# Hybrid decoder layer on one core: transposes of both heads in one row, next scores directly behind, filling steps regrouped

## Chip, core and metric

The kernel runs on one core of one Trainium2 chip. Its time is the device time of one execution in microseconds; several executions are taken and their median is compared. The profile is one execution recorded by the hardware profiler. TensorE is called PE in its rows, its weight loads PEld, VectorE DVE, ScalarE ACT, GpSimd POOL and SyncE, which issues the DMAs, SP.

## The reference

One decoder layer on x of 512 tokens by 1024 channels. The part that matters here is the stick-breaking attention with 8 heads of 64 channels, computed for blocks of 128 queries:

```
for blk in range(S // SB_BLOCK):
    z = jnp.einsum('bthd,bshd->bhts', qb, kb).astype(jnp.float32) * scale
    log_not = jnp.where(strict, jax.nn.log_sigmoid(-z), 0.0)
    suffix = lax.cumsum(log_not, axis=3, reverse=True) - log_not
    a = jnp.where(strict, jnp.exp(jax.nn.log_sigmoid(z) + suffix), 0.0)
    outs.append(jnp.einsum('bhts,bshd->bthd', a, vb))
...
merged = gates0 * (o_sb @ w_br_sb) + gates1 * (o_pool @ w_br_pool) + gates2 * (o_gm @ w_br_gm)
x = x + rms_norm(merged @ w_out, g_mix_post)
x = x + rms_norm(square(relu(rms_norm(x, g_ff_pre) @ w_ff_in)) @ w_ff_out, g_ff_post)
```

Two more mixers (pooling over trailing windows, gMLP gating), three sigmoid gates and a squared-ReLU MLP stand beside it.

## The kernel before, in words

Every float32 operand of a matrix product is cut into a high part (a cast on ACT, names such as whi, hT0, a) and a low part (a subtraction on DVE, wlo, hT1), and each product is three matmuls. One step of the generator `work` is such a product: three matmuls with 512 columns for most of it. `work` chains the projections of the other mixers (gating, pooling), the q and k projections of later head pairs and the gates. The DVE and ACT work that follows these products (win, pooled, pl, og, sg, kl) is issued when a step has been reached.

`attention` goes through 16 units: unit u is head pair u // 4 and query block i = u % 4, so unit 3 is the last block of head pair 0 and unit 4 the first of head pair 1. A unit passes four stages, for both heads of its pair:

- scores (`stick_scores`): four matmuls into two banks z; then on ACT sigmoids into nb and be, on POOL the causal masks, on DVE a reverse scan of nb and a product into be
- transposes (`stick_transpose`): i + 1 transposes of be by PE for each head into a bank pt; ACT casts pt to the high part of a, DVE subtracts for the low part
- values (`stick_values`): 2(i + 1) matmuls a by v into the bank av, of which there is one buffer
- sum: ACT copies the lower half of av to low, DVE adds it (low), and two DVE additions write the output of; both of these read av, so the next unit's values can't begin before they are done

In a pass of the loop the transposes of unit u - 1, the scores of unit u and the values of unit u - 1 are issued with steps of `work` between them (`fill`), in the numbers of FILLS. PE keeps the order of the program throughout. Ahead of attention, ACT and DVE are set free (`act.on = dve.on = False`): from there the scheduler of the framework puts their instructions in order from its own planning, and on the chip each engine then takes them in that fixed order. So the same edit can move instructions on ACT and DVE that it doesn't name.

The names in the rows are tiles; a helper records every operation, so nearly all rows have line 90.

Of the kernel before, what the change touches and what calls it, by code (L numbers as in the profile page):

```python
# [17 lines left out]
P = 128  # L18
T = 512
D = 1024  # L20
NT = T // P
# [9 lines left out]
AHEAD = 3  # L31
NO_SYNC = mybir.DependencyInfo(mybir.DependencyClass.NoSync, mybir.DependencyReason.DATA)
RAW, HL = 3, 6
FILLS = (2, 1, 3, 5)
LEAD = 36
WARM = 6

# [11 lines left out]
def trunk_layer(ctx: ExitStack, tc: tile.TileContext, x, w_in, w_pool, pool_scale, gm_gain,  # L49
# [27 lines left out]
    def slot(ring, name, dt=F32):  # L77
        return home[0].tile([P, T], dt, name=name, tag=ring, bufs=RINGS[ring])
# [19 lines left out]
    pe, act, dve, sp = (InOrder(e, True) for e in (nc.tensor, nc.scalar, nc.vector, nc.sync))  # L98

    def wide(name, dt=F32R):  # L100
        return sb.tile([P, 2 * T], dt, name=name, tag="wide", bufs=2)
# [153 lines left out]
    def split(src, hi, lo, scale=None):  # L255

        if scale is None:
            act.copy(hi, src)
            dve.tensor_sub(lo, src, hi.bitcast(F32))
        else:  # L260
            act.activation(hi, src, AF.Copy, scale=scale)
            dve.scalar_tensor_tensor(lo, src, scale, hi.bitcast(F32), ALU.mult,
                                           ALU.subtract)
# [68 lines left out]
    def bank(tag, name, dt=F32):  # L332
        return psum.tile([P, T], dt, name=name, tag=tag,
                         bufs={"mm": 3, "z": 2, "tr": 2, "av": 1}[tag])
# [23 lines left out]
    ident = cst.tile([P, P], F32, name="ident")  # L358
# [12 lines left out]
    if True:  # L371
# [31 lines left out]
        two, rs, hns, pts = {}, {}, {}, {}  # L403
        for step in V_ORDER.split():
            what = step.rstrip("0123")
            t, g = ([int(c) for c in step[len(what):]] + [0, 0])[:2]
# [56 lines left out]
        def stick_scores(hp, i):  # L463

            xq, kh, kl = qk[hp]
            n = (i + 1) * P
            tsl = slice(i * P, n)
            zs = [bank("z", "z") for _ in range(2)]
            for j in range(2):
                pe.matmul(zs[j][:, :n], lhsT=xq[j][:, tsl], rhs=kh[j][:, :n], start=True,  # L470
                                 stop=False)
            for j in range(2):
                pe.matmul(zs[j][:, :n], lhsT=xq[j][HALF[j], tsl], rhs=kl[HALF[j], :n],
                                 start=False, stop=True)
            res = []
            for j in range(2):
                nb, be = slot("nb", "nb"), slot("be", "be")
                act.activation(nb[:, :n], zs[j][:, :n], AF.Sigmoid, scale=-0.125)
                act.activation(be[:, :n], zs[j][:, :n], AF.Sigmoid, scale=0.125)

                for tile_, fill in ((nb, 1.0), (be, 0.0)):
                    nc.gpsimd.affine_select(tile_[:, n - P:n], tile_[:, n - P:n], [[-1, P]],  # L482
                                            ALU.is_ge, fill, base=-1, channel_multiplier=1)
                dve.tensor_tensor_scan(nb[:, :n][:, ::-1], nb[:, :n][:, ::-1],
                                             zeros.broadcast_to([P, n]), 1.0, ALU.mult, ALU.add)
                dve.tensor_mul(be[:, :n - 1], be[:, :n - 1], nb[:, 1:n])
                res.append(be)
            return res

        def stick_transpose(i, be):  # L490

            pt = bank("tr", "pt").rearrange("p (s t) -> p s t", s=NT)
            for s in range(i + 1):
                pe.transpose(pt[:, s, :], be[:, s * P:(s + 1) * P], ident)
            a = wide("a").rearrange("p (s a t) -> p s a t", s=NT, a=2)[:, :i + 1]
            split(pt[:, :i + 1, :], a[:, :, 0, :], a[:, :, 1, :])
            return a

        def stick_values(hp, i, parts, of):
            av = bank("av", "av").rearrange("p (j a t) -> p j a t", j=2, a=2)  # L500
            for j in range(2):
                hd = 2 * hp + j
                for s in range(i + 1):
                    vv = vT[s][hd // 4][:, hd % 4, :, :].rearrange("p a d -> p (a d)")
                    pe.matmul(av[:, j, :, :], lhsT=vv, rhs=parts[j][:, s, :, :],
                                     start=s == 0, stop=s == i)
            low = slot("tmp", "low")[:DH, :2 * P].rearrange("p (j t) -> p j t", j=2)
            act.copy(low, av[DH:P, :, 0, :])
            dve.tensor_add(low, av[0:DH, :, 0, :], low)
            for j in range(2):  # L510
                dve.tensor_add(of[HALF[j], i * P:(i + 1) * P], av[0:DH, j, 1, :],
                                     low[:, j, :])

        def attention(fill):

            units = [(hp, i) for hp in range(4) for i in range(NT)]
            be = parts = of = None
            for u in range(len(units) + 1):
                if u:
                    hp0, i0 = units[u - 1]  # L520
                    parts = []
                    for j in range(2):
                        parts.append(stick_transpose(i0, be[j]))
                        fill(FILLS[j])
                if u < len(units):
                    hp, i = units[u]
                    while qk[hp] is None:
                        fill(1)
                    be = stick_scores(hp, i)
                fill(FILLS[2])  # L530
                if u:
                    if i0 == 0:
                        of = slot("tmp", "of")
                    stick_values(hp0, i0, parts, of)
                    if i0 == NT - 1:
                        oT[hp0] = slot("out", "oh", F32R), slot("out", "ol", F32R)
                        split(of, *oT[hp0])
                fill(FILLS[3])


        wsr = slot("tmp", "wsr").rearrange("p (g t) -> p g t", g=4)
# [221 lines left out]
        def fill(n):  # L763
            for _ in range(n):
                next(work, None)
# [4 lines left out]
        pool_constants()  # L770
        fill(LEAD - LEAD // 2)
        attention(fill)
        run(work)
        for dd in range(KD // 2):
# [112 lines left out]
    parts = [None] * (FT // 2)  # L887
# [210 lines left out]
```

## Time and profile before

| | |
|---|---|
| median of 3 runs | 722.36 us (721.77 to 723.73) |
| the profiled execution | 722.87 us |
| its span, first to last instruction | 721.1 us |
| PE busy | 698.6 us, 97% |
| DVE busy | 494.0 us, 68% |
| ACT busy | 353.9 us, 49% |
| attention | from about 72 to 232 us of the span |

Times in rows are us from the start of the span. A timeline row has the start, the time until the end of the row's last instruction, the engine, the operation and its tiles (out<-in), the number of instructions, and in brackets the idle time of the engine before it with what ended it. Ends of matmuls are modelled, so two starts are compared rather than an end and a start.

### The profile page before, as it was taken

Reading aid. Unit: us, or ns where it says so; the run is one execution under the profiler, and the core shown is the slowest. Engines: PE = TensorE matmul, PEld = TensorE weight load, DVE = VectorE, ACT = ScalarE, POOL = GpSimd, SP = SyncE. Lnnn points to the kernel's source line nnn. Section 1 sums busy time; section 2 is a strip of 40 time slices with the busy share of each in tenths; the row PEclk is TensorE's granted clock in tenths of the full one; section 3 lists DMA queues with packets and bytes.
Section 4 is the critical chain, followed back from the end, with each engine's and each line's share of the span. In section 5 each row is a group of like instructions: output and inputs, shape, how many; then the busy total and the mean of one; then the engine's idle time right before and its main releaser. Section 6 shows DMA issues by size and latency. Waiting matters only on the chain.

```text
span 721.1 us, 9135 instructions
## 1 busy us (share of the span) xinstructions
PE 698.6 (97%) x3320; PEld 576.7 (80%) x3320; DVE 494.0 (68%) x771; ACT 353.9 (49%) x593; POOL 54.0 (7%) x106
## 2 busy tenths in 40 slices
PE   7999999999999999999999998999999999999994
PEld 4889887788888888888889777888888888888774
DVE  6745799777777544243576776747885679757897
ACT  6566666655444333321445654555534553445541
POOL 4100222111121000000040000000000000000001
PEclk9999999999999999999999999999999999999998
DMA  8272312322325233262325235633356234643543
GB/s 278 80 207 84 115 60 60 90 68 70 96 59 146 89 90 114 74 220 87 116 89 176 99 106 175 181 113 115 119 165 208 92 117 148 188 133 116 162 160 117
DMA packets 72432, 89.80 MB, mean 125 GB/s; under 512 B 4546, under 2 KB 49730, under 8 KB 72387
## 3 DMA queue, kind: packets, MB, share of 16 engines
q1 hardware_dynamic: 72384, 89.21, 39.5%
q8 instruction: 26, 0.43, 0.2%
q14 instruction: 20, 0.16, 0.1%
q10 hardware_dynamic: 2, 0.00, 0.0%
HBM read 85.01 MB, written 4.19 MB: 124 GB/s over the span
## 4 chain that ended last, share of the span: by engine, by line
PE 80%; DVE 10%; DMA 4%; ACT 3%; issue 2%; POOL 1%; SPq 0%; POOLq 0%; DVEq 0%; ACTq 0%
PE psc L90 25%; PE accf L90 18%; PE accx L90 7%; PE psb L90 6%; PE acc L90 6%; PE accz L90 5%; PE accy L90 4%; PE psv L90 3%; DMA raw<-in_w_ff_out_dram 3%; DVE wlo L90 2%; DVE ys L90 2%; PE psgv L90 2%; PE z L90 1%; PE av L90 1%; PE pt L90 1%
## 5 line engine op out<-in xcount | busy, mean ns | idle before, releaser
L90 DVE TENSOR_TENSOR wlo<-raw,whi 128x1024 fp32r<-128x1024 f32 (+1 forms) x145 | 158.1, 1095 | 109.6 <-ACT whi L90 108.8
L90 ACT CAST whi<-raw 128x1024 fp32r<-128x1024 f32 (+1 forms) x152 | 139.4, 927 | 140.5 <-PE psc L90 31.0
L90 PE MATMUL psc<-hT,whi 128*128 128x512 f32 x576 | 182.2, 398 | 0.0
L90 PE MATMUL accf<-hT,whi 128*128 128x512 f32 x448 | 138.1, 390 | 1.4 <-ACT rl L90 1.4
L90 PEld LDWEIGHTS psc<-hT,whi 128*128 128x128 f32 x576 | 103.9, 188 | 21.0 <-issue 1.5
L90 PE MATMUL psc<-hT,wlo 128*128 128x512 f32 x288 | 112.6, 391 | 0.0
L90 PEld LDWEIGHTS accf<-hT,whi 128*128 128x128 f32 x448 | 84.0, 188 | 19.1 <-ACT rl L90 1.8
L90 PE MATMUL accf<-hT,wlo 128*128 128x512 f32 x224 | 87.2, 389 | 0.0
L90 PEld LDWEIGHTS psc<-hT,wlo 128*128 128x128 f32 x288 | 54.1, 188 | 11.6
L90 PEld LDWEIGHTS accf<-hT,wlo 128*128 128x128 f32 x224 | 42.1, 188 | 8.8
L90 ACT CAST ah<-ec 128x768 fp32r<-128x768 f32 (+1 forms) x32 | 30.2, 944 | 32.6 <-DVE ec L90 32.1
L90 PE MATMUL accx<-whi,ah 128*128 128x512 f32 x96 | 37.9, 394 | 2.9 <-DVE ys L90 2.9
L284 POOL TENSOR_TENSOR pr<-pv,mhalf 128x1 f32<-128x1 f32 x8 | 4.8, 605 | 470.7 <-DVE pv L90 470.7
L90 DVE TENSOR_TENSOR al<-ec,ah 128x768 fp32r<-128x768 f32 (+1 forms) x32 | 34.8, 1087 | 4.7 <-ACT ah L90 4.5
L90 PE MATMUL accx<-wlo,ah 128*128 128x512 f32 x96 | 37.4, 390 | 0.0
L90 PE MATMUL accx<-whi,al 128*128 128x512 f32 x96 | 37.4, 390 | 0.0
L90 DVE TENSOR_TENSOR_SCAN nb<-nb,zeros 128x128 f32<-128x128 f32 (+3 forms) x32 | 27.5, 863 | 7.5 <-POOL nb L482 7.1
L90 DVE TENSOR_TENSOR ec<-ec 128x256 f32<-128x256 f32 x64 | 26.7, 421 | 7.0 <-ACT ec L90 6.7
L90 ACT CAST whi<-t 128x512 fp32r<-128x512 f32 x32 | 19.7, 616 | 14.8 <-DVE t L90 9.2
L90 PE MATMUL accy<-whi,al 128*128 128x512 f32 (+1 forms) x64 | 24.7, 386 | 1.9 <-DVE al L90 1.9
L90 ACT CAST a<-pt 128x128 fp32r<-128x128 f32 (+3 forms) x32 | 13.6, 426 | 25.9 <-PE pt L90 25.8
L90 ACT ACTIVATE sg<-psc 128x512 f32<-128x512 f32 x24 | 14.3, 598 | 22.7 <-PE psc L90 22.7
(197 smaller groups left out, 1236.0 us busy)
## 6 DMA issues: line engine op xcount, KB each, us to landing
raw<-in_w_ff_out_dram SPq DMA_DIRECT2D x96, 256.0 KB, 3.2
raw<-in_w_in_dram SPq DMA_DIRECT2D x42, 512.0 KB, 3.8
raw<-in_w_ff_in_dram SPq DMA_DIRECT2D x32, 512.0 KB, 3.9
xt<-in_x_dram SPq DMA_DIRECT2D x16, 256.0 KB, 6.3
raw<-in_w_out_dram SPq DMA_DIRECT2D x8, 512.0 KB, 3.7
raw<-in_w_ff_out_dram SPq DMA_DIRECT2D x8, 512.0 KB, 3.8
raw<-in_w_br_sb_dram SPq DMA_DIRECT2D x4, 512.0 KB, 3.4
x1d<-xt SPq DMA_DIRECT2D x8, 256.0 KB, 2.7
```

Of the source, the lines that this page charges most:

```text
L90: i = op(*args, **kw).ins
L284: nc.gpsimd.tensor_tensor(r, v, mhalf, ALU.pow)
```

## The change

FILLS has two numbers in place of four. The transposes of both heads are issued in a row, with no steps between them, and the scores of the next unit directly behind. Four steps stand between scores and values, where there were three, and seven behind the values, where there were five; a pass has 11 steps as before. Both banks pt are written before the casts and subtractions are issued. In the first pass, which has no transposes or values, 11 steps stand where there were 8.

```
-FILLS = (2, 1, 3, 5)
+FILLS = (4, 7)
...
-        def stick_transpose(i, be):
-
-            pt = bank("tr", "pt").rearrange("p (s t) -> p s t", s=NT)
-            for s in range(i + 1):
-                pe.transpose(pt[:, s, :], be[:, s * P:(s + 1) * P], ident)
-            a = wide("a").rearrange("p (s a t) -> p s a t", s=NT, a=2)[:, :i + 1]
-            split(pt[:, :i + 1, :], a[:, :, 0, :], a[:, :, 1, :])
-            return a
+        def stick_transposes(i, be):
+
+            pts = [bank("tr", "pt").rearrange("p (s t) -> p s t", s=NT) for _ in range(2)]
+            for j in range(2):
+                for s in range(i + 1):
+                    pe.transpose(pts[j][:, s, :], be[j][:, s * P:(s + 1) * P], ident)
+            res = []
+            for pt in pts:
+                a = wide("a").rearrange("p (s a t) -> p s a t", s=NT, a=2)[:, :i + 1]
+                split(pt[:, :i + 1, :], a[:, :, 0, :], a[:, :, 1, :])
+                res.append(a)
+            return res
...
-                    parts = []
-                    for j in range(2):
-                        parts.append(stick_transpose(i0, be[j]))
-                        fill(FILLS[j])
+                    parts = stick_transposes(i0, be)
...
-                fill(FILLS[2])
+                fill(FILLS[0])
...
-                fill(FILLS[3])
+                fill(FILLS[1])
```

On PE, around the transposes of unit 3 (pt, four per head) and the scores of unit 4 (z), the order before has three matmuls psc, which are one step, on both sides of the second head's transposes:

```order
L90 MATMUL psc<-hT_142,whi 128x512
L90 MATMUL psc<-hT_143,whi 128x512
L90 MATMUL psc<-hT_142,wlo 128x512
L90 MATMUL pt<-ident,be 128x128 x4
L90 MATMUL psc<-hT_142,whi 128x512
L90 MATMUL psc<-hT_143,whi 128x512
L90 MATMUL psc<-hT_142,wlo 128x512
L90 MATMUL z<-kh,xq 128x128 x2
L90 MATMUL z<-kl,xq 128x128 x2
```

The same place in the changed kernel:

```order
L90 MATMUL psc<-hT_142,whi 128x512
L90 MATMUL psc<-hT_143,whi 128x512
L90 MATMUL psc<-hT_142,wlo 128x512
L90 MATMUL pt<-ident,be 128x128 x8
L90 MATMUL z<-kh,xq 128x128 x2
L90 MATMUL z<-kl,xq 128x128 x2
```

The three steps that stood behind the transposes of head 0 now stand ahead of them; the scores keep their place among the steps, and the values of unit 3 come four steps behind them instead of three.

On DVE, before, from the pooling work (pooled) onward: low and of with av_1186 in them are the sum of unit 2; a_1246 and a_1263 are the transposed weights of unit 3; pl, win and wlo belong to the pooling mixer and to the weights:

```order
L90 SCALAR_TENSOR_TENSOR pooled_1216<-win_1176,tok_937 64x512 x2
L90 TENSOR_TENSOR low_1193<-av_1186,low_1193 64x256
L90 TENSOR_TENSOR pooled_1216<-first_1219,tok_937 128x16
L90 TENSOR_TENSOR of_951<-av_1186,low_1193 64x128 x2
L90 TENSOR_TENSOR a_1246<-pt_1241,a_1246 128x4x128
L90 TENSOR_TENSOR pl_1223<-pooled_1216,ph_1222 128x512
L90 TENSOR_TENSOR win_1235<-tok_1008 128x511
L90 COPY win_1235<-tok_1008 128x1
L90 TENSOR_TENSOR a_1263<-pt_1258,a_1263 128x4x128
L90 TENSOR_TENSOR wlo_1452<-raw_1211,whi_1451 128x1024
L90 TENSOR_TENSOR win_1255<-win_1235 128x510
```

In the changed kernel the pair pooled (64x512) is followed by pooled (128x16), pl, win (128x511) and its one-column copy, and then by these rows, where the sum of unit 2 has av_1214 in it, a_1263 and a_1266 are unit 3's, and nb_1275 and nb_1285 are the two scans of unit 4:

```order
L90 TENSOR_TENSOR wlo_1452<-raw_1199,whi_1451 128x1024
L90 TENSOR_TENSOR win_1247<-win_1235 128x510
L90 COPY win_1247<-win_1235 128x2
L90 TENSOR_TENSOR kl_1297<-psc_1194,kh_1295 128x512
L90 TENSOR_TENSOR low_1221<-av_1214,low_1221 64x256
L90 TENSOR_TENSOR a_1263<-pt_1253,a_1263 128x4x128
L90 TENSOR_TENSOR a_1266<-pt_1254,a_1266 128x4x128
L90 SCALAR_TENSOR_TENSOR nb_1275<-nb_1275,zeros_138 128x128
L90 TENSOR_TENSOR win_1317<-win_1247 128x508
L90 COPY win_1317<-win_1247 128x4
L90 SCALAR_TENSOR_TENSOR nb_1285<-nb_1285,zeros_138 128x128
L90 TENSOR_TENSOR of_954<-av_1214,low_1221 64x128 x2
```

The pair of unit 2 that last reads av stood directly behind pooled; it now stands behind pl, wlo, kl, both a of unit 3, the win chain and both scans of unit 4.

On ACT, before, at the same place (xq and kh are casts for the q and k of a later head pair, ph is the high part of pooled):

```order
L90 COPY low_1193<-av_1186 64x256
L90 CAST xq_1199<-psc_1108 64x512
L90 COPY xq_1198<-ql_1200 64x512
L90 COPY xq_1199<-ql_1200 64x512
L90 CAST a_1246<-pt_1241 128x4x128
L90 CAST ph_1222<-pooled_1216 128x512
L90 CAST a_1263<-pt_1258 128x4x128
L90 CAST whi_1451<-raw_1211 128x1024
L90 CAST kh_1295<-psc_1206 128x512
```

and in the changed kernel:

```order
L90 CAST xq_1187<-psc_1108 64x512
L90 COPY xq_1186<-ql_1188 64x512
L90 COPY xq_1187<-ql_1188 64x512
L90 CAST ph_1210<-pooled_1204 128x512
L90 CAST whi_1451<-raw_1199 128x1024
L90 CAST kh_1295<-psc_1194 128x512
L90 COPY low_1221<-av_1214 64x256
L90 CAST a_1263<-pt_1253 128x4x128
L90 CAST a_1266<-pt_1254 128x4x128
```

The copy low of unit 2 moved from ahead of xq to behind kh, and both casts a of unit 3 stand behind it.

## Rows read from the trace of the kernel before

**Rows 1.** The page: span, and busy time by engine.
```profile
span 721.1 us, 9135 instructions
PE 698.6 (97%) x3320; PEld 576.7 (80%) x3320; DVE 494.0 (68%) x771; ACT 353.9 (49%) x593; POOL 54.0 (7%) x106
```

**Rows 2.** What PE waited for in the run: us in total, times, longest.
```profile
PE accx L90 <- DVE ys L90: 2.9, 2, 2.0
...
PE pt L90 <- DVE be L90: 0.4, 1, 0.4
PE av L90 <- DVE a L90: 0.2, 1, 0.2
```

**Rows 3.** Busy time in one stretch: us, PE, PEld, DVE, ACT, POOL, clock, DMA.
```profile
113.43:119.84 6.41, 6.19 (x31) 5.12 (x30) 6.41 (x13) 4.74 (x11) 2.30 (x4) 1.00 0.21 54
```

**Rows 4.** Timeline of PE around unit 3, and the values of unit 15.
```profile
111.41 0.60 PE L90 MATMUL pt<-ident,be 128*128 128x128 f32 x4
...
112.55 0.33 PE L90 MATMUL z<-kh,xq 128*128 128x128 f32 x2
...
115.24 0.63 PE L90 MATMUL av<-a,v 128*128 128x256 f32 x4
...
116.67 0.62 PE L90 MATMUL psc<-hT,whi 128*128 128x512 f32 x2
...
119.84 0.39 PE L90 MATMUL psc<-hT,wlo 128*128 128x512 f32 x1
120.59 0.30 PE L90 MATMUL pt<-ident,be 128*128 128x128 f32 x1 [0.36 <-DVE be L90]
...
230.74 1.12 PE L90 MATMUL av<-a,v 128*128 128x256 f32 x8
231.69 0.40 PE L90 MATMUL psb<-plh,whi 128*128 128x512 f32 x1
```

**Rows 5.** Timeline of DVE around the sum of unit 2.
```profile
110.94 1.38 DVE L90 SCALAR_TENSOR_TENSOR pooled<-win,tok 64x512 f32<-64x512 f32 x2
112.35 0.42 DVE L90 TENSOR_TENSOR low<-av,low 64x256 f32<-64x256 f32 x1
112.69 0.16 DVE L90 TENSOR_TENSOR pooled<-first,tok 128x16 f32<-128x16 f32 x1
112.80 0.58 DVE L90 TENSOR_TENSOR of<-av,low 64x128 f32<-64x128 f32 x2
113.43 0.69 DVE L90 TENSOR_TENSOR a<-pt,a 128x512 fp32r<-128x512 f32 x1
...
119.84 0.41 DVE L90 TENSOR_TENSOR low<-av,low 64x256 f32<-64x256 f32 x1
```

**Rows 6.** Timeline of ACT in the same stretch.
```profile
111.54 1.25 ACT L90 CAST xq<-ql 64x512 fp32r<-64x512 f32 x2
...
113.42 0.62 ACT L90 CAST ph<-pooled 128x512 fp32r<-128x512 f32 x1
...
114.43 1.05 ACT L90 CAST whi<-raw 128x1024 fp32r<-128x1024 f32 x1
```

**Rows 7.** Timeline of POOL: the mask of unit 4's second nb.
```profile
117.97 0.29 POOL L482 TENSOR_SCALAR_AFFINE_SELECT nb<-nb 128x128 f32<-128x128 f32 x1
```

**Rows 8.** Timeline of PE at the start of the run.
```profile
1.79 2.74 PE L90 MATMUL warm<-warm 128*128 128x512 bf16 x6 [1.79 <-DVE warm L90]
...
6.90 0.65 PE L90 MATMUL trx<-ident,hn 128*128 128x128 f32 x4 [0.27 <-DVE hn L90]
10.35 0.74 PE L90 MATMUL psv<-whi,hT 128*128 128x512 f32 x2 [2.79 <-ACT hT L90]
```

**Rows 9.** Busy time at the run's end, columns as in the third group.
```profile
711.75:715.10 3.35, 0.00 (x0) 0.00 (x0) 3.35 (x11) 1.02 (x4) 0.55 (x1) 1.00 0.62 239
715.20:721.00 5.80, 0.00 (x0) 0.00 (x0) 2.10 (x5) 0.00 (x0) 0.55 (x1) 0.50 0.48 181
```

**Rows 10.** Timeline of DVE: the second head's weights of unit 15.
```profile
229.66 0.68 DVE L90 TENSOR_TENSOR a<-pt,a 128x512 fp32r<-128x512 f32 x1
```

## Prediction

> **What bounds the kernel now.** I read the page first: PE is busy for 698.6 us of a span of 721.1 [rows 1], so the time is PE's, and an edit counts only by what it does to PE's idle time or to the number and pace of its matmuls. Then the waits of PE: in the whole of attention there are two, on be by the transposes and on a by the values, 0.4 and 0.2 us [rows 2]. The others lie ahead of attention or behind it, the largest in the MLP. Then the timeline around these two, which lie close together at units 3 and 4 [rows 4]. The reader is to see what PE waits for there: DVE. From 113.43 to 119.84 DVE works 6.41 us of 6.41, 13 instructions without a gap [rows 3]. DVE is idle for a third of the run, but not here, where pooling windows, q and k of the next head pair and the attention's own work meet. What a change of order costs is read from this stretch.
>
> **PE's own work.** No matmul is added or removed. From the second head's transposes to the scores is 112.55 - 111.41 = 1.14 us and holds four transposes and one step [rows 4]. A step comes from the 14 matmul starts between 116.67 and 119.84: 3.17 / 14 = 0.226 each, 0.68 for three [rows 4]. So four transposes cost 0.46, and they cost that between two steps already, with a transpose before and a step behind. No row has a transpose ahead of scores or of another head's transpose; a switch could cost or save up to one transpose's place, 0.46 / 4 = 0.11 us, in each of 16 units, 1.8 us either way. I take nothing, since the four already stand at one pace.
>
> **What moves on PE.** In steps counted from the start the scores keep their place, the transposes of head 0 come three steps later, those of head 1 one step later, and the values one step later: 3 steps behind the scores became 4, and the scores 3 steps behind head 0 became none. For be there is more time, 2.0 and 0.7 us. For a of head 0 there is less, 2 steps or 1.4 us; for head 1 there is the same, but its cast and subtraction now queue behind head 0's.
>
> **What that saves.** The wait at unit 4's transposes: 120.59 - 119.84 = 0.75 us where a matmul start costs 0.23, so 0.52 lost. The wait between the two heads' values in unit 3: 116.67 - 115.24 = 1.43 us for the eight matmuls that take 231.69 - 230.74 = 0.95 in unit 15, so 0.48 lost [rows 4]. Together 1.00 us, the most that the edit can win in attention; with the waits gone PE has nothing else there to lose.
>
> **What it adds: the bank av.** There is one buffer av. Unit 3's values may start only after DVE has done both additions of of unit 2, which read av. Before, these stood directly behind low and were done at 112.80 + 0.58 = 113.38 [rows 5], 1.9 us ahead of the values at 115.24. In the changed order they are moved behind both scans of unit 4, and each engine takes its instructions in order. I walk it with rows. Everything up to the pooled pair stands as before, and ends at 110.94 + 1.38 = 112.32. pooled 128x16 (0.16) ends at 112.48. pl needs ph from ACT: ACT finishes the two xq at 111.54 + 1.25 = 112.79, and ph takes 0.62 [rows 6], so pl starts at about 113.43, and DVE is idle for 0.95 us, which it was not before. The weight cast whi follows ph and takes 1.05, until 114.5, while DVE has pl and two window instructions to do; no wait taken there. From pl to the pair of, DVE has pl, win, copy, wlo, win, copy, kl, low, both a, a scan, win, copy, a scan. Without low these are the same 13 forms that filled 113.43 to 119.84, 6.41 us [rows 3, 5]; low adds 112.69 - 112.35 = 0.34. POOL's mask for the second scan was done at 118.26 [rows 7]; the sigmoids of unit 4 come out a few tenths later than before, and the second scan is due at 119.9, so it doesn't wait. of begins at 113.43 + 6.75 = 120.18 and ends at 120.76; with a few hundredths for the signal, the values start at about 120.8.
>
> PE is due there at 115.24 + 0.68 = 115.92. **It waits 4.9 us.** Both a of unit 3 are done over a microsecond before of, so this wait takes the place of the one on a. Queued behind the values on PE are seven steps, the transposes of unit 4 and all that follows: nothing can go past. The be of unit 4 stands directly behind of on DVE, and its transposes are due at 120.8 + 0.95 + 7 x 0.68 = 126.5, so that saving stands.
>
> **Bounds of the wait.** If pl did not wait for ph, of would end 0.95 earlier: 3.95 us. If each of 14 instructions paid its whole length instead of overlapping with the next, as low does with 0.42 against 0.34 [rows 5], 1.1 more: 6.0 us. I take 4.9: the 13 forms ran at that pace back to back before, and the cast that pl waits for stands behind the same xq casts as before.
>
> **The other units.** In each of them the changed order has of directly behind low, or with only pooling work between, and ahead of the next unit's a, so av is free long before. The tightest for a is unit 15: its second a began at 229.66, behind wlo and sg [rows 10]; now both stand behind these, and end at about 229.66 + 2 x 0.65 = 230.95, while the values come at 230.74 + 0.68 = 231.42 [rows 4]. No wait, with 0.5 us or more to spare. Behind attention the order of every engine is the same; on SP one load of a gain for the MLP's norm stands one weight chunk later, far ahead of its use.
>
> **Sum.** +4.9 - 1.0 = +3.9 us on the profiled execution's 722.87: 726.8. That execution lies 0.51 above the median of the runs, 722.36, so 726.3 against the median; with the bounds of the wait, 725.3 to 727.4.
>
> **Rivals.** *The clock falls in the new wait.* At the run's end PE has nothing to do from 711.75; the granted clock reads 1.00 until 715.10 and 0.50, 1.2 of 2.4 GHz, from 715.20 [rows 9]. The wait of 2.79 us at 10.35 stands between matmuls of full pace on both sides. A wait of 4.9 us is longer than the idle time after which the clock fell at the end, so it may fall here; that it fell once says not that it does each time. Price: at the start six matmuls with 512 columns took 2.74 us, 0.46 each where 0.23 is usual, and the pace was full at 6.90 at the latest, so the slow pace lasted 2.7 to 5.1 us [rows 8], which costs half of that, 1.4 to 2.6, middle 1.9: 728.2 us. The Trainium skill (TensorE: Matmul & The Clock Gate, section Why this matters for your kernels) warns that an idle gap in the middle of a kernel sends the clock back to half rate. By that warning the sum would be 728.2 rather than 726.3; the end of this trace agrees, the 2.79 us wait shows no such thing.
>
> *Not slower: av is no bottleneck.* If the printed order were not what holds PE, or DVE got to of before the values are due, the two waits go and nothing comes: 722.36 - 1.0 = 721.4, within 0.3%. It decides at a wait of 3.2 us: below that, the loss less the 1.0 stays under 2.2 us, 0.3% of the time, which is about what a measurement of this kernel can tell from no change. DVE would have to finish of by 119.1, 1.7 us sooner than the walk. For it speaks only that DVE's idle 0.95 may not occur; that alone leaves 3.95.
>
> *Given back later.* The MLP's waits, 2.9 us on ys for accx the largest group [rows 2], would swallow the delay if they hung on something that does not move with PE. They hang on DVE work that reads PE's own results, so they move along. Were I wrong, 722 us or so.
>
> **Chances.** The wait of 4 to 6 us with the clock kept, 726.3: 0.52. The same with the clock down, 728.2: 0.31. Not slower by av being free, 721.4: 0.08. Given back later, about 722: 0.04. A wait of 3.2 us or less that ends between, or pace effects of the transposes of over a microsecond, shared out: 0.05. Slower by over 0.3% (above 724.5): 0.87; within 0.3%: 0.11; faster: 0.02, which would need the 1.0 us and most of the 1.8 us of pace. The range goes from just under the low end of the likeliest case to near the high end of the clock's, 725.2 to 729.0, with a tenth left out on each side.
>
> **What would show it.** Right: one wait of PE of four to six us ahead of the first av of unit 3, near 116, released by DVE's of; no wait on be at unit 4; DVE idle nearly a microsecond ahead of pl; the granted clock of 115 to 128 tells the rival. Wrong: unit 3's values starting before 119; a second wait in attention of over half a microsecond; PE's busy sum changed with the same count; or waits in the MLP shorter by microseconds.

## The result: 0.8% slower, and the profile after

The changed kernel takes 730.44 us, median of 6 runs (727.08 to 732.44), where the kernel before takes 723.05 in the 6 runs beside and ahead of it (720.87 to 726.53). The ratio is 1.0083, with an interval of 1.0059 to 1.0108; the ratios on record are not the quotients of the medians, which is 1.0102 here. The direction is as predicted, but 730.44 lies above the range of 725.2 to 729.0.

The profiled execution of the changed kernel took 727.08 us, so it is the shortest of the six. Its page, beside [rows 1]:

```profile
span 725.3 us, 9132 instructions
PE 700.8 (97%) x3320; PEld 578.8 (80%) x3320; DVE 492.7 (68%) x771; ACT 353.3 (49%) x593; POOL 52.0 (7%) x106
```

PE's busy sum rose by 2.2 us with the same number of matmuls, so besides the new wait matmuls became slower somewhere. The waits of PE:

```profile
PE av L90 <- DVE of L90: 4.7, 1, 4.7
PE accx L90 <- DVE ys L90: 2.7, 3, 1.5
```

The two waits in attention, on be and on a [rows 2], are gone. One wait of 4.7 us stands in their place, released by of on DVE. The timeline of PE at unit 3, to lay beside [rows 4]:

```profile
111.96 0.42 PE L90 MATMUL z<-kh,xq 128*128 128x128 f32 x2
...
115.18 0.39 PE L90 MATMUL psc<-hT,wlo 128*128 128x512 f32 x1
120.24 1.84 PE L90 MATMUL av<-a,v 128*128 128x256 f32 x8 [4.67 <-DVE of L90]
121.88 1.05 PE L90 MATMUL psc<-hT,whi 128*128 128x512 f32 x2
122.74 0.63 PE L90 MATMUL psc<-hT,wlo 128*128 128x512 f32 x1
```

And DVE over the same time, where [rows 5] had of directly behind low and the short pooled:

```profile
111.92 0.18 DVE L90 TENSOR_TENSOR pooled<-first,tok 128x16 f32<-128x16 f32 x1
113.02 0.69 DVE L90 TENSOR_TENSOR pl<-pooled,ph 128x512 fp32r<-128x512 f32 x1 [0.93 <-ACT ph L90]
...
116.70 0.40 DVE L90 TENSOR_TENSOR low<-av,low 64x256 f32<-64x256 f32 x1
117.03 1.27 DVE L90 TENSOR_TENSOR a<-pt,a 128x512 fp32r<-128x512 f32 x2
...
119.21 0.41 DVE L90 TENSOR_TENSOR_SCAN nb<-nb,zeros 128x128 f32<-128x128 f32 x1
119.54 0.55 DVE L90 TENSOR_TENSOR of<-av,low 64x128 f32<-64x128 f32 x2
120.13 0.49 DVE L90 TENSOR_TENSOR be<-be,nb 128x127 f32<-128x127 f32 x2
```

DVE idles 0.93 us ahead of pl, then works without a gap, and gets to of behind both scans. Both a end at 117.03 + 1.27 = 118.30, also late. PE had been due at 115.18 + 0.23 = 115.41, and the first head's values need the first a alone, which ends at about 117.03 + 0.69 = 117.72 (0.69 is one such subtraction in [rows 5]). So in this order of DVE's work a wait of about 2.3 us on a would have stood there even with av free. The prediction's DVE walk counts from a start of unit 4's scores at 112.55; in this execution they start at 111.96, 0.59 earlier. So its 120.8 is 120.2 here; 120.24 was measured.

The granted clock changes behind the wait. Stretches of the changed kernel (columns as in the third group of rows: length, PE, PEld, DVE, ACT, POOL, clock, DMA):

```profile
115.50:120.24 4.74, 0.07 (x1) 0.03 (x1) 4.70 (x14) 2.98 (x9) 1.04 (x4) 1.00 0.39 111
...
120.50:123.85 3.35, 3.35 (x13) 2.96 (x13) 2.59 (x7) 0.37 (x1) 0.00 (x0) 0.50 0.00 0
...
124.20:127.60 3.40, 3.40 (x16) 2.77 (x15) 2.20 (x7) 1.74 (x3) 0.00 (x0) 1.00 0.02 5
```

The granted clock reads 1.00 throughout the wait. It reads 0.50, 1.2 of 2.4 GHz, once PE is at work again, and 1.00 again after that.

How much of the loss lies in attention is read from the views of two tiles: the first start of z, which is the first scores, and the first start of psf, which is a matmul behind attention. The columns are the shortest, middle and longest duration in ns, then the first and the last start. Before:

```profile
L90 PE MATMUL z<-kh,xq x32: 220/310/398, 72.2 to 218.6; 128*128 128x128 f32 x8, 128*128 128x256 f32 x8, 128*128 128x384 f32 x8, 128*128 128x512 f32 x8
L90 PE MATMUL psf<-hT,whi x128: 277/283/364, 371.6 to 398.3; 128*128 128x256 f32 x128
```

After:

```profile
L90 PE MATMUL z<-kh,xq x32: 220/351/475, 71.7 to 223.2; 128*128 128x128 f32 x8, 128*128 128x256 f32 x8, 128*128 128x384 f32 x8, 128*128 128x512 f32 x8
L90 PE MATMUL psf<-hT,whi x128: 278/283/363, 376.1 to 402.8; 128*128 128x256 f32 x128
```

From z to psf is 371.6 - 72.2 = 299.4 us before and 376.1 - 71.7 = 304.4 after: 5.0 us more. I call this the stretch z to psf below. Behind it, to the end of the span, are 349.5 and 349.2 us.

### The profile page after: what moved, and what is told of

The parts are those of the page before. It is cut to its first block, busy times and chain, and to the rows that moved or that the text cites. A ratio compares the mean times of both kernels' runs of the same rounds, so it can differ in the third digit from the quotient of the medians.

```text
span 725.3 us, 9132 instructions
## 1 busy us (share of the span) xinstructions
PE 700.8 (97%) x3320; PEld 578.8 (80%) x3320; DVE 492.7 (68%) x771; ACT 353.3 (49%) x593; POOL 52.0 (7%) x106
## 4 chain that ended last, share of the span: by engine, by line
PE 78%; DVE 12%; DMA 5%; ACT 3%; issue 1%; SPq 1%; POOL 0%; POOLq 0%; DVEq 0%; ACTq 0%
PE psc L90 25%; PE accf L90 18%; PE accx L90 6%; PE psb L90 6%; PE acc L90 6%; PE accz L90 4%; PE accy L90 3%; DMA raw<-in_w_ff_out_dram 3%; DVE wlo L90 3%; PE psv L90 3%; PE psgv L90 2%; DVE ys L90 1%; PE av L90 1%; PE z L90 1%; DVE al L90 1%
## 5 line engine op out<-in xcount | busy, mean ns | idle before, releaser
L90 PEld LDWEIGHTS psc<-hT,whi 128*128 128x128 f32 x576 | 106.3, 189 | 22.7 <-issue 1.5
L90 PE MATMUL acc<-whi,mh 128*128 128x512 f32 x64 | 25.1, 392 | 0.0
```

The source lines that it names most:

```text
L90: i = op(*args, **kw).ins
```

## Experiments

The theory: the wait for the bank av costs what it lasts, and the clock that falls with it costs several us more. Its rivals: the clock's part is small or none; the order on PE, with transposes in a row, is slower in itself; the delay is made up behind attention. The kernels of one group ran on one chip and share runs of the kernel before: medians of 721.68 us in the first group, 722.86 in the second, 720.76 in the third. Losses in us below are differences of medians.

**The changed kernel again** (c1_after in the first group, c2_after in the third), without an edit.

> The changed kernel once more, beside the kernel before on one chip. Theory A (the wait of the values of unit 3 for the sum of unit 2, 4.7 us, costs 3.9 us net, and in it the clock falls in nearly every run, for 3.4 us or more of half pace): 4.5 to 9 us over before, spread over several us from run to run, granted clock of the runs 0.986 to 0.992. Theory B (the clock falls only now and then, and the far runs were the chip's): about 3.9 us over before in the median, clock above 0.992.

> The changed kernel a third time, beside the two kernels with matmuls in the place of the wait, all on one chip. Theory A (3.3 us of PE's attention lost without the clock, and the clock's fall on top): 2 to 4 us over both of them, granted clock 0.986 to 0.992.

726.95 us, ratio 1.0072 (1.0054 to 1.0091), and 726.94 us, ratio 1.0080 (1.0060 to 1.0100). Both have the 4.7 us wait at av. The stretch z to psf takes 304.9 and 305.6 us, 5.5 and 6.2 more than before; the medians lie 5.3 and 6.2 us over the kernel before, so this stretch holds about the whole loss of these two. In these executions the clock fell earlier, before PE had resumed, and for twice as long. First c1_after, whose values start at 121.52, then c2_after, whose values start at 120.07:

```profile
119.30:126.00 6.70, 4.48 (x15) 3.93 (x16) 5.68 (x17) 0.94 (x2) 0.00 (x0) 0.50 0.07 23
126.20:129.60 3.40, 3.40 (x18) 2.75 (x16) 1.70 (x4) 1.74 (x3) 0.00 (x0) 1.00 0.00 0
```

```profile
119.35:126.10 6.75, 6.03 (x18) 5.17 (x19) 5.22 (x16) 1.47 (x3) 0.00 (x0) 0.50 0.01 2
```

So the low clock lasts about 3.4 us in one execution and about 6.8 in another, and a part of it can fall into the wait, where PE has nothing to lose: PE works 4.48 us of it in c1_after and 6.03 in c2_after.

**PE kept at work in the wait** (e2_busy_wait, first group; e8_busy_wait_2, the same kernel, third group): the changed kernel with 20 matmuls ahead of unit 3's values, into a bank that nobody reads.

```
 # stick attention, u == 4, ahead of stick_values
+if u == 4:
+    spare = bank("mm", "spare")
+    for _ in range(20):
+        pe.matmul(spare, lhsT=hT[0][:, 0, :P], rhs=hT[0][:, 0, :], start=True, stop=True)
```

> The changed kernel with 20 matmuls of 512 columns, whose result nobody reads, issued ahead of the values of unit 3; all of the reference is computed. They take 20 x 0.227 = 4.5 us, about what PE waits there. Theory A: PE has no wait over 0.6 us at the values, the granted clock stays 1.00 through the stretch, and the time is 3.5 to 4.5 us over before with a narrow spread, 2 to 4 us under the changed kernel. Theory B, that the excess over 3.9 us has nothing to do with the clock in this wait: the time is that of the changed kernel, 6 to 7 us over before.

> The changed kernel with 20 matmuls ahead of the values of unit 3, again. It came out at 1.1 us over before on one chip, where PE's attention is 3.4 us longer. Theory N (what lies between is the MLP's waits, that differ from chip to chip and execution to execution): level within 0.7 us with the kernel before that has the same 20 matmuls. Theory G (the changed order gives something back in the MLP that the order before does not): 1 us or more under it.

722.84 us, ratio 1.0015 (1.0003 to 1.0026), and 723.04 us, ratio 1.0033 (1.0020 to 1.0047). The timeline of PE and the clock in e2_busy_wait:

```profile
116.04 4.70 PE L90 MATMUL spare<-hT 128*128 128x512 f32 x20
120.88 1.19 PE L90 MATMUL av<-a,v 128*128 128x256 f32 x8
```

```profile
116.04:120.88 4.84, 4.70 (x22) 3.60 (x20) 4.79 (x14) 3.09 (x9) 1.04 (x4) 1.00 0.35 108
120.88:127.00 6.12, 6.12 (x32) 5.22 (x33) 5.39 (x14) 2.11 (x4) 0.00 (x0) 1.00 0.01 3
```

The values start 120.88 - 116.04 = 4.84 us after the extra matmuls begin, so they are as late as in the changed kernel, yet the clock stays at 1.00. On the same chip this is 726.95 - 722.84 = 4.1 us, and 726.94 - 723.04 = 3.9 us, less than the changed kernel. In the stretch z to psf it takes 302.8 us in both, 3.4 more than before and 2.1 to 2.8 less than c1_after and c2_after. So the rival of a small clock falls: the values start equally late, and where PE works in place of the wait the clock stays up and the stretch is 2.1 to 2.8 us shorter.

The size fits too. At half pace about half of the low time in which PE works is lost: an estimate of 3.35 / 2 = 1.7 us for the first profile of the changed kernel, 4.48 / 2 = 2.2 for c1_after and 6.03 / 2 = 3.0 for c2_after. Measured over 302.8 are 1.6, 2.1 and 2.8.

The rest of the 4 us is not shown to be the clock's. Behind the stretch c1_after takes 725.5 - 377.9 = 347.6 us and c2_after 725.1 - 377.1 = 348.0, where e2_busy_wait has 345.9 and e8_busy_wait_2 346.4. That is 1.6 to 1.7 us, and in all four profiles the clock stays at 1.00 there until PE's work is done. So theory A of e2_busy_wait holds for the clock and for the gap to the changed kernel, but its 3.5 to 4.5 us over before came out as 1.2.

**The late sum alone** (e3_before_late_of, first group): the kernel before, with the two additions of of unit 2 issued behind the scores of unit 4 and ordered behind its last scan on DVE.

```
-for j in range(2):
-    dve.tensor_add(of[...], av[0:DH, j, 1, :], low[:, j, :])
+def sum_up():
+    for j in range(2):
+        dve.tensor_add(of[...], av[0:DH, j, 1, :], low[:, j, :])
+if (hp, i) == (0, 2):
+    return sum_up
+sum_up()
...
 be = stick_scores(hp, i)
+if u == 4:
+    dve.floor, floor = scans[-1], dve.floor
+    late()
+    dve.floor = floor
```

> The kernel before, with the two additions of of unit 2 alone put behind the scans of unit 4 on DVE; transposes and steps as before. Theory A: the same wait at the values of unit 3, 3.5 to 4.5 us, the waits on a and be there gone, so 2.5 to 3.5 us over before with the clock kept and 4 to 7 with the clock down. Rival C (the grouped transposes and the regrouped steps cost it, on PE, not the sum's place): within 1 us of before.

729.25 us, ratio 1.0094 (1.0077 to 1.0111): 7.6 us over before, which is the loss of the change or a little more, with transposes and steps placed as before. The stretch z to psf takes 377.2 - 71.5 = 305.7 us. The waits of PE, the timelines of PE and DVE and the clock:

```profile
PE av L90 <- ACT kh L90: 4.5, 1, 4.5
```

```profile
119.19 1.19 PE L90 MATMUL av<-a,v 128*128 128x256 f32 x4 [4.49 <-ACT kh L90]
```

```profile
117.84 0.72 DVE L90 TENSOR_TENSOR_SCAN nb<-nb,zeros 128x128 f32<-128x128 f32 x2
118.49 0.55 DVE L90 TENSOR_TENSOR of<-av,low 64x128 f32<-64x128 f32 x2
```

```profile
118.20:124.90 6.70, 5.71 (x18) 4.87 (x19) 5.83 (x19) 2.63 (x6) 0.00 (x0) 0.50 0.19 65
```

The wait is put down to a cast kh on ACT. But the values start at 119.19, 0.15 behind the end of of at 118.49 + 0.55 = 119.04, and this is the same distance as in the changed kernel (119.54 + 0.55 = 120.09, then 120.24); and of is all that the edit moves. Both a stand in their old places on DVE here, ahead of wlo and kl. So the late sum by itself is enough for the wait, for the fall of the clock and for a loss as large as that of the change.

**The sum early, with the new order** (e4_windows_8, first group) **and with the old one** (e5_before_windows_8, second group): the pooling windows' DVE work is issued at each eighth step of the q and k projections and of a gate instead of each third. PE's order is untouched.

```
-alongside(chain(qk_pair(2), gate_of(1, 0)), pool_windows(), 3),
+alongside(chain(qk_pair(2), gate_of(1, 0)), pool_windows(), 8),
```

> The changed kernel with the pooling windows' DVE work issued at every eighth step instead of every third; PE's order is instruction for instruction that of the changed kernel, and on DVE the sum of unit 2 stands ahead of wlo, kl and a. Theory A: no wait over 0.6 us at the values of unit 3, no wait on be, clock kept: 0.5 to 1.5 us under before. Rival C (PE's new order costs it): still 4 us or more over before.

> The kernel before with the pooling windows issued at every eighth step, the transposes and fills as before. Rival D (grouped transposes save something on PE that the wait hid): at least 0.5 us slower than the changed kernel with the windows at every eighth step. Theory A (grouping is worth nothing by itself, only the two waits of 1.0 us are): 0.7 to 1.5 us under before, level with that kernel.

e4_windows_8: 720.54 us, ratio 0.9982 (0.9968 to 0.9996), the only kernel whose interval lies below 1. e5_before_windows_8: 722.42 us, ratio 0.9989 (0.9972 to 1.0006). DVE and PE in e4_windows_8:

```profile
112.54 0.41 DVE L90 TENSOR_TENSOR low<-av,low 64x256 f32<-64x256 f32 x1
112.87 0.16 DVE L90 TENSOR_TENSOR first<-win,inv 128x16 f32<-128x16 f32 x1
112.98 0.58 DVE L90 TENSOR_TENSOR of<-av,low 64x128 f32<-64x128 f32 x2
```

```profile
112.75 1.03 PE L90 MATMUL pt<-ident,be 128*128 128x128 f32 x8
113.54 0.42 PE L90 MATMUL z<-kh,xq 128*128 128x128 f32 x2
...
116.99 1.11 PE L90 MATMUL av<-a,v 128*128 128x256 f32 x8
```

With of close behind low again, one short instruction between them, the values start 116.99 - 113.54 = 3.45 us after the scores, without a wait; in the changed kernel this was 120.24 - 111.96 = 8.28. The stretch z to psf takes 297.9 us here and 298.4 in e5_before_windows_8, against 299.4 before. So the two old waits are worth 299.4 - 298.4 = 1.0, and the transposes in a row about 0.5 us over 16 units. Unit 3 alone points the same way: its eight transposes take 113.54 - 112.75 = 0.79 us to the scores, where twice the 0.46 of the prediction is 0.92. The two kernels ran on different chips, and each stretch is one profile; the 0.5 is at the edge of what rival D asked for. The rival of a slower order falls.

**The same 20 matmuls in the kernel before** (e6_before_busy, second group; e9_before_busy_2, the same kernel, third group), to see whether the new order has a price that e2_busy_wait keeps.

> The kernel before with 20 matmuls of 512 columns ahead of the values of unit 3, whose result nobody reads: 4.54 us more work of PE, with no wait. The waits on a and be behind it go, 1.0 us, so attention ends about 3.5 us later, with the clock kept. Theory G: 1.5 to 2.5 us over before, since the MLP's waits give back 1 to 2 us. Theory N: 3.2 to 4.2 us over before.

> The kernel before with 20 matmuls ahead of the values of unit 3, again, on the same chip. Theory N: 1.5 to 3.3 us over before, level within 0.7 us with the changed kernel that has the same 20 matmuls. Theory G: 1 us or more above that.

726.05 us, ratio 1.0029 (1.0011 to 1.0047), and 722.55 us, ratio 1.0021 (1.0004 to 1.0039). The medians lie 3.2 and 1.8 us over before, within theory N both times. The stretch z to psf takes 302.8 us in both, as in e2_busy_wait. On the third chip 722.55 and 723.04 stand side by side: the new order has no price of its own there either.

**The kernel before again** (b1_before, second group), as a measure of what a ratio means.

> The kernel before itself, for a second profile of it and for what the comparison gives between equal kernels. All theories: within 0.3% of before. Theory G (an attention that ends later is partly given back by shorter waits in the MLP): from the last values to the last matmul 479 to 480 us again, as in the first profile. Theory N (that stretch only varies from execution to execution): 475 to 479.

722.55 us, ratio 1.0001 (0.9975 to 1.0026), stretch z to psf 299.4. From the last values to the last matmul are 478 us where the first profile has 480, which is theory N: the part behind attention varies by 2 us between executions of one kernel.

**Half the matmuls** (e7_busy_10, second group): e2_busy_wait with `range(10)`, so that a wait of about half the length stays.

> The changed kernel with 10 such matmuls ahead of the values of unit 3, 2.27 us, which leaves PE a wait of about 2.4 us there. If the clock falls only in a wait of 3.4 us or more, as at the run's end: granted clock 1.00 in the stretch, time that of the kernel with 20 matmuls, 0.5 to 2 us over before on this chip. If a shorter wait is enough: 2 us or more above that kernel, with the clock at 0.50 for a part of 118 to 127.

726.18 us, ratio 1.0033 (1.0013 to 1.0053). Its wait and its stretches:

```profile
PE av L90 <- DVE of L90: 2.4, 1, 2.4
```

```profile
117.60:119.90 2.30, 0.00 (x0) 0.00 (x0) 2.25 (x8) 0.68 (x2) 0.00 (x0) 1.00 0.35 124
119.95:121.30 1.35, 1.35 (x10) 1.31 (x11) 1.29 (x5) 0.12 (x1) 0.00 (x0) 1.00 0.07 12
121.35:124.70 3.35, 3.35 (x10) 2.60 (x9) 2.78 (x9) 0.87 (x3) 0.00 (x0) 0.50 0.00 0
```

After a wait of 2.4 us the clock fell in this execution: 1.4 us after PE had resumed, and for the shorter of the two times. The stretch z to psf takes 304.4 us, 1.6 more than with 20 matmuls. In the medians this doesn't show: 726.18 stands beside 726.05 of e6_before_busy on the same chip, and the intervals of the ratios overlap almost wholly. So neither expectation came out whole: the clock fell, and the time is that of 20 matmuls. In how many runs it falls after 2.4 us, one profile doesn't show.

## Why the prediction missed

- **The saved waits, 1.0 us:** right. Both waits are gone, and removing them alone, in e5_before_windows_8, is worth 1.0 in the stretch z to psf.
- **The new wait, 4.9 us:** right in place and cause, 4.7 measured, and the walk along DVE met the start of av within 0.1 us once the earlier scores are counted in. e3_before_late_of shows that the late of alone makes it.
- **Transposes in a row, 0 taken:** about 0.5 us saved, inside the bounds of 1.8 either way.
- **Net without the clock, +3.9:** +3.4 in the stretch z to psf, from e2_busy_wait and e8_busy_wait_2 (302.8 against 299.4). 4.8 of wait less 1.0 less 0.5 gives 3.3.
- **The clock: the step that failed.** It stood as a rival with a chance of 0.31, on the grounds that it fell once, at the run's end [rows 9], and not around the 2.79 us wait [rows 8]; the likeliest case, at 0.52, had the clock kept. It was down in all four profiles that have a wait of 4.5 us or more here (the changed kernel three times, e3_before_late_of), and it kept 1.00 where 20 matmuls filled the wait. The mean granted clock is 0.986 to 0.994 in the changed kernel's 18 runs and 0.993 to 0.997 in the 22 of e2_busy_wait and e8_busy_wait_2. It should have been the likeliest case. The Trainium skill's warning that the prediction names (TensorE: Matmul & The Clock Gate, section Why this matters for your kernels) was the better guide here, and these four profiles agree with it.
- **The clock's price, 1.4 to 2.6, middle 1.9:** a little small. It was read from six matmuls at the start, a single low time. In the stretch z to psf the fall took 1.6, 2.1 and 2.8 us in the three profiles of the changed kernel, the most in c2_after, where the clock was low for 6.8 us and PE worked in 6.03 of them. With 2.1 to 2.8 the net is 3.4 + 2.1 = 5.5 and 3.4 + 2.8 = 6.2 us over before, which is what c1_after and c2_after lose by their medians, 5.3 and 6.2. The prediction's own sum would have been 728.4 to 729.1. The 4.1 and 3.9 us by which the 20 matmuls beat the changed kernel are not all the clock's price: the part behind the stretch, 1.6 to 1.7 us, has no low clock in it. The second fall that c1_after shows, at 10 us, lies ahead of everything that the edit touches.
- **Not slower because av is free:** wrong, but e4_windows_8 is that case. There the new order does win the 1.0 us that the rival gave it and 0.5 more in the stretch z to psf.
- **Given back later, 0.04:** too low for a part of it. e2_busy_wait, e8_busy_wait_2 and e9_before_busy_2 lose 3.4 us in the stretch z to psf and only 1.2 to 2.3 in the medians (722.84 - 721.68, 723.04 - 720.76, 722.55 - 720.76). In their profiles the part behind the stretch takes 345.9, 346.4 and 345.6 us where the kernel before has 349.5 and, in b1_before, 347.4. One wait in it is that on ys, 1.1 or 1.2 us in these three where the kernel before has 2.9 [rows 2] and 2.3. Why it is shorter was not settled; since one kernel's own executions differ by 2 us there, single profiles can't decide it. e6_before_busy, with 348.3 and 3.2 us in the medians, shows nothing of the kind.

Open too is why the first six runs of the changed kernel lie at 730.44 and the later twelve at 726.9. Against the kernel before beside them the losses are 7.4, 5.3 and 6.2 us; the last two are accounted for above, the first is 1.2 to 2.1 us more. About 0.7 us of 730.44 is the kernel before itself, 723.05 beside these runs where the prediction started from 722.36. These two parts together carry 730.44 over the range. By the ratios the three groups hardly differ, 1.0083, 1.0072 and 1.0080 with intervals that overlap almost wholly, so the 1.2 to 2.1 us may be scatter. Five of the first six runs have a mean granted clock of 0.986 to 0.989, the later twelve 0.989 to 0.994; a mean of 0.988 instead of 0.991 over 728 us is 2 x 0.003 x 728 = 4.4 us more at half clock, worth up to 2.2. Where those falls stood, no profile shows: the only one profiled of the six, at 727.08, is the fastest. So the cause of this part stays open.

## What to carry to other kernels

When an edit moves work on one engine only, look at where the scheduler then puts the instructions that free a single-buffered bank: two short additions, set behind other work on DVE, cost more here than all that the edit could save. Price a new idle time of TensorE of several us as itself plus a fall of the clock, take the fall as the likely case, and count half of the low time in which TensorE works, here 1.7 to 3.0 us. And where the order is good but a late release spoils it, move the filling work of the releasing engine (here one number, 3 to 8) before giving the order up.

## What the runs showed of the hardware that was not expected

- The clock fell after PE was back at work: in the changed kernel's profile within 0.3 us of its resuming (0.50 from 120.50), in e7_busy_10 1.4 us after it, having read 1.00 through the whole wait. In c1_after, c2_after and e3_before_late_of it fell within the wait.
- It came back after about 3.4 or about 6.8 us with the same kernel and the same wait, so one profile doesn't give the price of a fall.
- The clock can fall elsewhere, after shorter waits. e4_windows_8, whose attention has no wait, shows two falls in its profile:

```profile
10.85:14.20 3.35, 3.35 (x12) 2.77 (x10) 3.35 (x4) 1.90 (x4) 2.11 (x2) 0.50 0.93 351
430.70:437.40 6.70, 6.70 (x24) 5.41 (x23) 5.63 (x10) 4.42 (x8) 0.00 (x0) 0.75 0.46 154
```

The second row's 0.75 is half of the stretch at half clock. Both stand just behind waits that the kernel before has as well: 1.96 us on hT at the start, ended at 10.13, and 1.84 us on al in the MLP, ended at 429.65. In the kernel before's profile these waits last 2.79 [rows 8] and 1.56 us, and the clock reads 1.00 behind both. So in these profiles the length of a wait alone doesn't tell whether a fall follows.
